# Second-direction operators and input matrices built in attention, S5 states summed before the output product, gates stored as a row

## Chip, cores and metric

One core of one Trainium2 chip runs the whole model in one launch. Times are device microseconds of that core; where runs are named, the number is the median of several executions of the same program.

## What is computed

The reference is a two-layer hybrid backbone over 1024 latent tokens and 256 context tokens of width 1024. `c` and `c_ctx` are two conditioning vectors; each layer turns both into shift, scale and gate (`ada_mod`).

```python
for layer in range(2):
    shift_x, scale_x, gate_x = ada_mod(c, ada_w[layer], ada_b[layer])        # silu(c) @ w + b, three parts
    shift_c, scale_c, gate_c = ada_mod(c_ctx, ada_w[layer], ada_b[layer])
    hx = rms_norm(x) * (1 + scale_x) + shift_x                                # hc likewise from the context
    if layer % 2 == 0:
        oc, ox = even_mixer(hc, hx, ...)   # grouped-query attention beside a bidirectional RG-LRU
    else:
        oc, ox = odd_mixer(hc, hx, ...)    # bidirectional grouped S5, then a GLU
    x = x + gate_x * ox
    if layer == 0:
        xc = xc + gate_c * oc
return rms_norm(x, final_norm_w)

def s5_direction(u, ab, bb, c, h0, reverse):          # 64 groups of 16 channels, 64 complex states each
    bu = einsum('blgj,gpj->blgp', u, bb)               # real and imaginary part
    s_re, s_im = complex_scan(ab, bu, h0, reverse)
    return einsum('blgp,gjp->blgj', s_re, c_re) - einsum('blgp,gjp->blgj', s_im, c_im)
```

`bb` (the input matrix) is the discretised `b`: `bb_re = f_re*b_re - f_im*b_im`, `bb_im = f_re*b_im + f_im*b_re`. The S5 runs forward and backward (d = 0 and 1), and the outputs are added.

## The kernel before

The projections and the output products work on float32 values that are split into a high and a low part (names ending in `h` and `l`, or `hh`, `hl`, `whi`, `wlo`), with three matmuls each. The kernel passes through these stages:

1. Norm, modulation and S5 parameters (to about 95 us).
2. Layer 0's input projections with the RG-LRU (about 95 to 405 us). TensorE's program order there is written out by hand in the string `PJ` (L857), a list of jobs with a number of steps each: `u` (RG-LRU input of a channel block), `r` (its gate matrices), `q` (queries, keys and values), `g` (gate path) and `a`, the modulation matrices of both layers (`ada`, L206). `ada` goes over eight chunks of 512 columns. A chunk is eight matmuls of 128x32 by 128x512 that fall in turn on four column groups of the array; between two of them TensorE may be given to other jobs. The result goes to SBUF as `admr`, and `part2` of the chunk before runs when two matmuls of the next are done. For a gate chunk `part2` multiplies `admr` with `selb`, which selects one condition and copies its row to 128 partitions, adds the bias on VectorE (`gt_g`) and stores 128 equal rows in `gd`; for layer 0 it does so once for each of the two conditions, out of a PSUM tag with two buffers that the chunks' sums share.
3. Attention (about 476 to 836 us): 16 units (two halves of the heads for each of eight query tiles) of ten key tiles, 160 iterations in all, every engine's program order written by hand. In an iteration TensorE transposes the exponentials (`tp`), ScalarE copies them to `pth`, VectorE makes `ptl`, TensorE multiplies with the values (`av`). `score_gen` makes the next unit's scores. Between these, steps of other generators are run: `post` (gate, output projection, residual `xr`, norm) and, from unit 2 on, two steps of `tg`, the generator `operators` on GpSimd. For each of eight channel groups f it makes the rotation tables of both directions (`tab_gen`: 8 blocks a group, each with two sums, whose halves are copied in reversed order into the same tile by GpSimd, L1238 and L1240) and the output operators `ca` of direction 0 (`op_gen`: two of 128x576 a group, three instructions each), and stores them to DRAM. The norm of a finished query tile (`norm_gen`, L1125) takes the rsqrt by Newton steps on GpSimd and multiplies `xr` by it on GpSimd (`xn`), then TensorE transposes `xn`.
4. The transition: weight splits and the input product of layer 1.
5. The S5 loop (L1880 on), f = 0 to 7, in it i = 0 to 7 for direction i // 4 and a pair of channel groups i % 4. TensorE's stream is filled with the next group's `u` and the `g` products (`fm`). `v_mm` multiplies `U` (read back from DRAM after a reordering store `usd`) with the input operator; `rot` (VectorE) turns `v` by the tables into `t1`, turns the scanned `z` of the step before back into the state `st` of two halves, and scans; `y_mm` multiplies `tm` with `U` and both halves of both directions' states with the operators `ca`. `x_gen` makes the next group's input matrix `xe`, `x2` on VectorE, `c_gen` the operators `ca` of direction 1 on VectorE, `c_sign` a sign on ScalarE; direction 0's `ca` are loaded by `c_load`.
6. GLU, output projection and final norm.

SP issues the DMAs; outside the hand-ordered blocks a scheduler orders them, and inside they stand where the code puts them. Helper `tt` (L77) records all two-tensor operations, so these are told apart by their tiles.

## Time and profile before

| | us |
|---|---|
| runs | 1480.28, 1482.72, 1492.19 (median 1482.72) |
| profiled execution | 1477.37 |
| its span, first to last instruction | 1475.6 |

The granted TensorE clock was 0.969 of full speed over the span. A row of the profile gives an engine's busy time; PE is the matmul stream of TensorE, PEld its weight loads (which overlap), DVE is VectorE, ACT ScalarE, POOL GpSimd, SP the engine that issues the DMAs. In rows of groups, `out<-in` names the tiles, then come shapes, count, busy time with the mean in nanoseconds, and the idle time of the engine just before them with what ended it.

### The profile page before, as it was taken

Reading aid. Unit: us, or ns where it says so; the run is one execution under the profiler, and the core shown is the slowest. Engines: PE = TensorE matmul, PEld = TensorE weight load, DVE = VectorE, ACT = ScalarE, POOL = GpSimd, SP = SyncE. Lnnn points to the kernel's source line nnn. Section 1 sums busy time; section 2 is a strip of 40 time slices with the busy share of each in tenths; the row PEclk is TensorE's granted clock in tenths of the full one; section 3 lists DMA queues with packets and bytes.
Section 4 is the critical chain, followed back from the end, with each engine's and each line's share of the span. In section 5 each row is a group of like instructions: output and inputs, shape, how many; then the busy total and the mean of one; then the engine's idle time right before and its main releaser. Section 6 shows DMA issues by size and latency. Waiting matters only on the chain.

```text
span 1475.6 us, 22202 instructions
## 1 busy us (share of the span) xinstructions
PE 1358.0 (92%) x7680; PEld 1117.8 (76%) x7680; DVE 1057.3 (72%) x2302; ACT 785.8 (53%) x1397; POOL 365.9 (25%) x576
## 2 busy tenths in 40 slices
PE   4699869999998999999999789999999999999996
PEld 1477648688886777887777677888888878888885
DVE  7576784878675877788887769999999983332235
ACT  4757865784656655656666445555555652222222
POOL 1030000000102488888985300000000000101153
PEclk8899979999999999999999999999999989999998
DMA  8343325444215444445432567778777873232412
GB/s 304 128 156 120 102 69 162 133 154 129 70 42 162 109 132 134 137 124 143 124 112 86 187 179 217 222 211 222 203 211 214 247 203 125 64 94 79 143 58 86
DMA packets 213153, 213.78 MB, mean 145 GB/s; under 512 B 47792, under 2 KB 170288, under 8 KB 212784
## 3 DMA queue, kind: packets, MB, share of 16 engines
q1 hardware_dynamic: 213040, 212.36, 48.3%
q8 instruction: 61, 1.00, 0.3%
q14 instruction: 52, 0.43, 0.1%
HBM read 147.89 MB, written 64.42 MB: 144 GB/s over the span
## 4 chain that ended last, share of the span: by engine, by line
PE 56%; DVE 17%; ACT 8%; issue 8%; POOL 6%; DMA 5%; SPq 0%; DVEq 0%; POOLq 0%; ACTq 0%
PE fm L1409 13%; PE fm L193 4%; PE fm L195 4%; PE fm L194 4%; PE tp L936 3%; PE v L1409 2%; PE v L1636 2%; PE op L1682 2%; PE wps L1409 2%; PE y L1682 2%; PE pS L914 2%; POOL xo L77 2%; DVE S L917 2%; PE op L1105 2%; PE op L1109 2%
## 5 line engine op out<-in xcount | busy, mean ns | idle before, releaser
L937 ACT ACTIVATE pth<-tp 128x512 fp32r<-128x512 f32 x160 | 95.4, 598 | 118.5 <-PE tp L936 114.2
L77 POOL TENSOR_TENSOR zl<-sgl,zh 128x512 fp32r<-128x512 f32 x8 | 10.4, 1296 | 477.7 <-DMA wst<-in_glu_w 377.6
L77 DVE TENSOR_TENSOR ptl<-tp,pth 128x512 fp32r<-128x512 f32 x160 | 109.5, 686 | 25.8 <-ACT pth L937 25.2
L1409 PE MATMUL fm<-hh,whi 128*128 128x512 f32 (+1 forms) x312 | 119.5, 383 | 2.7 <-ACT ut L1584 2.7
L1409 PE MATMUL fm<-hl,whi 128*128 128x512 f32 (+1 forms) x312 | 119.9, 384 | 1.0 <-POOL hl L77 1.0
L1409 PE MATMUL fm<-hh,wlo 128*128 128x512 f32 (+1 forms) x312 | 117.3, 376 | 0.0
L195 PE MATMUL fm<-hh,wlo 128*128 128x512 f32 (+1 forms) x288 | 104.1, 361 | 6.6 <-DVE wlo L77 6.6
L193 PE MATMUL fm<-hh,whi 128*128 128x512 f32 (+1 forms) x288 | 106.2, 369 | 3.2 <-DVE sg L548 1.8
L936 PE MATMUL tp<-ident,S 128*128 128x128 f32 x672 | 101.9, 274 | 5.6 <-DVE q L77 2.1
L77 DVE TENSOR_TENSOR wlo<-wst,whi 128x512 fp32r<-128x512 f32 x98 | 68.5, 721 | 52.1 <-ACT whi L1402 41.3
L194 PE MATMUL fm<-hl,whi 128*128 128x512 f32 (+1 forms) x288 | 103.8, 361 | 1.0 <-DVE hl L487 0.9
L936 PEld LDWEIGHTS tp<-ident,S 128*128 128x128 f32 x672 | 82.6, 140 | 29.2 <-ACT S L925 2.8
L925 ACT ACTIVATE S<-S,mx 128x1280 f32<-128x1280 f32 (+1 forms) x80 | 95.2, 1190 | 9.4 <-DVE S L917 9.3
L917 DVE TENSOR_SCALAR_CACHE_REDUCE S<-pS,mx 128x512 f32<-128x512 f32 (+1 forms) x128 | 78.4, 614 | 21.4 <-PE pS L915 13.7
L914 PE MATMUL pS<-k,q 128*128 128x512 f32 (+1 forms) x208 | 82.7, 402 | 11.7 <-DVE S L917 11.0
L175 POOL CAST v<-vs 128x256 fp32r<-128x256 f32 x5 | 2.1, 417 | 321.4 <-DMA gd<-gt_g 290.5
L193 PE MATMUL fm<-whi,hh 128*128 128x256 f32 x240 | 70.7, 295 | 2.5 <-ACT up L669 2.5
L915 PE MATMUL pS<-k,q 128*128 128x512 f32 (+1 forms) x208 | 71.5, 351 | 0.0
L944 PE MATMUL av<-pth,v 128*128 128x512 f32 x160 | 71.0, 444 | 0.0
L194 PE MATMUL fm<-wlo,hh 128*128 128x256 f32 x240 | 68.9, 287 | 1.4 <-DVE wlo L77 1.4
L193 PEld LDWEIGHTS fm<-hh,whi 128*128 128x128 f32 x288 | 55.7, 193 | 18.7 <-issue 4.6
L1409 PEld LDWEIGHTS fm<-hh,whi 128*128 128x128 f32 x312 | 60.0, 192 | 11.7 <-ACT ut L1584 3.0
(494 smaller groups left out, 4130.7 us busy)
## 6 DMA issues: line engine op xcount, KB each, us to landing
adw<-in_ada_w SPq DMA_DIRECT2D x48, 512.0 KB, 4.7
tab<-tabd SPq DMA_DIRECT2D x64, 320.0 KB, 5.1
tabd<-tab SPq DMA_DIRECT2D x64, 160.0 KB, 2.6
wst<-in_ev_w_in SPq DMA_DIRECT2D x36, 256.0 KB, 3.2
wst<-in_od_w_in SPq DMA_DIRECT2D x32, 256.0 KB, 4.2
tmd<-ks SPq DMA_DIRECT2D x16, 512.0 KB, 4.8
wst<-in_glu_w SPq DMA_DIRECT2D x32, 256.0 KB, 2.8
usd<-ut SPq DMA_DIRECT2D x8, 768.0 KB, 4.7
```

The costliest lines, as they stand in the source:

```text
L77: e.tensor_tensor(o, a, b, op=op)
L193: T.matmul(ps, l[0], r[0], start=first, stop=False)
L194: T.matmul(ps, l[0], r[1], start=False, stop=False)
L195: T.matmul(ps, l[1], r[0], start=False, stop=last)
L914: T.matmul(pS[:, :n], q1[:, a], k1[:, h, c0:c0 + n], start=True, stop=False)
L915: T.matmul(pS[:, :n], q2[:, a], k1[:, h, c0:c0 + n], start=False, stop=True)
L917: V.tensor_scalar(P[a][:, c0:c0 + n], pS[:, :n], -0.125, prev[a], op0=ALU.mult, op1=ALU.min, accum_out=mx[:, a, b:b + 1])
L925: S.activation(s, s, AF.Exp, bias=nb, scale=-1.0, accum_out=sm)
L936: T.transpose(ps[:, 128 * a:128 * a + 128], P[a][:, 128 * kt:128 * kt + 128], ident)
L937: S.activation(parts[0], ps, AF.Copy)
L944: T.matmul(av, v2[:, kt, h], pt[0], start=first, stop=False)
L1409: T.matmul(ps, w[k][a], r(k, b), start=k == 0 and i == 0, stop=k == 7 and i == 2)
```

## The change

- Gates as a row: one matmul with `sel` gives both conditions' rows; `gd` holds one row each, which the loads copy to 128 partitions (`gB`, `g1`). `selb` is gone. `ada` has four weight buffers in place of two and loads four ahead; `part2` of a chunk runs after all eight matmuls of the next; in `PJ` the `a` steps of a chunk stand together as `a:10`.
- Attention: GpSimd's `operators` now makes `ca` of both directions and, in a new `x_gen(f)`, the input matrices of both directions, stored in `xd`. The reversed halves of the tables are made on ScalarE by `mirror()`, at the earliest two iterations after the sum. `xn` of the norm is made by ScalarE. `t_split` takes the high part of the RG-LRU's product on ScalarE for the later units and stands two iterations behind the load. `tg` gets three steps instead of two in four of a unit's ten iterations.
- S5: `c_gen`, `c_sign` and `x_gen` are gone; `xe`, `x2` and all four `ca` are loaded. In `rot` VectorE adds the two halves of the state into `sb` and `y_mm` has one matmul in place of two for each direction.

Both halves of a state were multiplied with the same operator, so their sum can be taken before the product.

```diff
-    gd = dr.tile([3, 128, D], F32, name="gd")
+    gd = dr.tile([3, D], F32, name="gd")
...
-            for cond in range(2 - l):
-                ps = pp.tile([128, 512], F32, name="gt_p", tag=tag, bufs=pb)
-                T.matmul(ps, selb[:, cond], m, start=True, stop=True)
-                g = pq.tile([128, 512], F32, name="gt_g", tag="sg")
-                tt(V, g, ps, bb, ALU.add)
...
-                Q.dma_start(gd[2 * l + cond, :, c], g)
+            n = 2 - l
...
+            ps = pp.tile([128, 512], F32, name="gt_p", tag=tag, bufs=pb)[0:n]
+            T.matmul(ps, sel[:, 0:n], m, start=True, stop=True)
+            tt(V, g, ps, bb, ALU.add)
...
+            Q.dma_start(gd[2 * l:2 * l + n, c], g)
...
-                if prev is not None and h == 1:
+                if prev is not None and kk == 7:
                     part2(*prev)
...
-    jobs = dict(a=ada(prg, pgp, [(0, 4), (0, 5), (1, 0), (1, 4), (1, 1), (1, 2), (1, 3), (1, 5)], 2, "ad", 2, 2))
+    PJ = ("u0:26 u1:26 r0:1 q0:2 r0:2 q0:2 r0:1 q0:2 u2:16 r0:4 a:11 r0:5 u2:3 q0:8 r1:1 u2:1 q0:16 u2:5 r1:6 q0:8 r1:3 a:10 "
+          "q0:8 r1:2 u2:1 r1:1 r2:1 q0:21 r2:2 q0:14 a:10 u3:24 g0:5 r2:3 u3:2 r2:1 g0:2 r2:3 g0:5 a:10 g0:13 g1:8 r2:2 "
...
+    jobs = dict(a=ada(prg, pgp, [(0, 4), (0, 5), (1, 0), (1, 4), (1, 1), (1, 2), (1, 3), (1, 5)], 2, "ad", 4, 4))
...
-    Q.dma_start(gB, gd[0:2].rearrange("c p n -> p c n"))
+    Q.dma_start(gB, gd[0:2].unsqueeze(0).to_broadcast([128, 2, D]))
...
+    def t_split(X, e=S):
+        split(*X["mr"], X.pop("rn"), e, G)
...
-            tt(G, xn, xr, r.to_broadcast([128, D]), ALU.mult)
-            for _ in range(NW):
+            yield
+            S.activation(xn, xr, AF.Copy, scale=r)
+            for _ in range(NW - 1):
                 yield
...
             tt(G, o, o, tb, op)
-            r = tab[:, :, c, 0:80][:, :, ::-1]
-            if c:
-                G.tensor_scalar(r, o, -1.0, None, op0=ALU.mult)
-            else:
-                G.tensor_copy(r, o)
+            mirrors.append((now[0] + 2, tab, c, None if c == 0 else (d, f, q)))
...
+    def mirror():
+
+        while mirrors and mirrors[0][0] <= now[0]:
+            _, tab, c, to = mirrors.pop(0)
+            S.activation(tab[:, :, c, 0:80][:, :, ::-1], tab[:, :, c, 80:160], AF.Copy, scale=-1.0 if c else 1.0)
...
-    def op_gen(f, PP, c, h):
+    def op_gen(f, d, PP, c, h):
...
+    def x_gen(f):
...
+        for i, op in enumerate((ALU.add, ALU.subtract)):
+            tt(G, x[:, i], bc[:, i], (FR, FRs)[i], ALU.mult)
+            tt(G, t, bc[:, 1 - i], (FIs, FI)[i], ALU.mult)
+            yield
+            tt(G, x[:, i], x[:, i], t, op)
+            if i:
+                Q.dma_start(xd[f].rearrange("p a n -> p (a n)"), x.rearrange("p a d g c -> p (a d g c)"))
+            yield
...
+            for d in range(2):
...
+                for h in range(2):
+                    yield from tab_gen(f, E, M, d, h)
+                    if h == 0:
+                        G.tensor_scalar(c[:, 0], c[:, 0], sgp, -1.0, op0=ALU.mult, op1=ALU.mult)
+                    yield from op_gen(f, d, PP, c, h)
+            yield from x_gen(f)
...
-                    run(tg, 2)
+                    mirror()
+                    run(tg, 2 + (i % 3 == 0))
...
-        def x_gen(X, e):
...
-        def c_gen(X, h):
-            X["CA"][1, h] = ca = pg.tile([128, 4, 9, 16], F32, name="ca", tag="ca", bufs=6)
-            return cprod(ca, X["PP"], 1, h, slice(8, None, -1), X["c"][:, 0], X["c"][:, 1], ALU.subtract, 2)
...
-                X0["St"][p0, d0] = s = pg.tile([128, 2, 2, 128], F32, name="st", tag=f"st{d0}", bufs=3 if d0 else 4)
+                s = pg.tile([128, 2, 2, 128], F32, name="st", tag="st", bufs=2)
                 tt(V, s if d0 == 0 else s[:, :, :, ::-1], zz[:, :, :, 31:159], tab0, ALU.mult)
+                X0["St"][p0, d0] = o = pg.tile([128, 2, 128], F32, name="sb", tag=f"sb{d0}", bufs=3 if d0 else 6)
+                tt(V, o, s[:, 0], s[:, 1], ALU.add)
...
-                    for c in range(2):
-                        T.matmul(y[:, i], ca.rearrange("p t c -> p (t c)"), St[p, d][:, c, i], start=False, stop=d + c == 2)
+                    T.matmul(y[:, i], ca.rearrange("p t c -> p (t c)"), St[p, d][:, i], start=False, stop=d == 1)
...
                 if i < 2:
-                    ck = c_gen(X, i)
-                elif 2 < i < 7:
+                    c_load(X, 1, i)
+                if 2 < i < 7:
```

## Rows read from the trace of the kernel before

**Rows 1.** The page, busy time of each engine (share of span, instructions).

```profile
PE 1358.0 (92%) x7680; PEld 1117.8 (76%) x7680; DVE 1057.3 (72%) x2302; ACT 785.8 (53%) x1397; POOL 365.9 (25%) x576
```

**Rows 2.** Windows: stretch, length, busy PE, PEld, DVE, ACT, POOL, clock, DMA share, GB/s.

```profile
95.00:217.00 122.00, 99.06 (x535) 79.87 (x533) 91.94 (x156) 82.36 (x100) 0.00 (x0) 0.90 0.35 112
217.00:405.00 188.00, 181.03 (x1112) 148.07 (x1112) 134.49 (x256) 117.94 (x182) 4.52 (x8) 0.98 0.42 129
502.00:826.00 324.00, 311.41 (x1750) 253.79 (x1748) 253.14 (x633) 192.52 (x339) 254.92 (x459) 1.00 0.41 117
973.27:1014.99 41.72, 41.72 (x282) 36.52 (x281) 39.83 (x85) 23.33 (x53) 0.00 (x0) 1.00 0.76 217
```

**Rows 3.** TensorE's instructions in time near 217 us: start, us, [wait before].

```profile
217.06 2.07 PE L235 MATMUL gt_p<-admr,selb 128*128 128x512 f32 x2 [9.60 <-DVE gt_g L77]
```

**Rows 4.** TensorE's instructions in time, 255 to 290 us.

```profile
259.43 1.06 PE L255 MATMUL adps<-adw,scc 128*32 128x512 f32 x8
...
276.09 1.04 PE L255 MATMUL adps<-adw,scc 128*32 128x512 f32 x2
```

**Rows 5.** TensorE's groups by shape, 95 to 405 us.

```profile
L255 PE MATMUL adps<-adw,scc 128*32 128x512 f32 x128 | 26.4, 638 | 0.6 <-DMA adw<-in_ada_w 0.6
...
L235 PE MATMUL gt_p<-admr,selb 128*128 128x512 f32 x12 | 7.8, 737 | 11.1 <-DVE gt_g L77 11.1
```

**Rows 6.** GpSimd's groups by shape, 455 to 880 us.

```profile
L77 POOL TENSOR_TENSOR tab<-EEf,MMf 128x160 f32<-128x160 f32 x64 | 29.7, 464 | 0.0
...
L77 POOL TENSOR_TENSOR cb<-cb,ct 128x576 f32<-128x576 f32 x16 | 22.8, 1428 | 1.0
L1238 POOL TENSOR_SCALAR tab<-tab 128x160 f32<-128x160 f32 x32 | 20.0, 625 | 2.8
L77 POOL TENSOR_TENSOR cb<-PPa,bca 128x576 f32<-128x576 f32 x16 | 19.2, 1203 | 0.0
...
L77 POOL TENSOR_TENSOR xn<-xr,rs_yn 128x1024 f32<-128x1024 f32 x8 | 15.2, 1894 | 0.0
...
L1240 POOL COPY tab<-tab 128x160 f32<-128x160 f32 x32 | 10.1, 317 | 2.0
```

**Rows 7.** Waits, 476 to 836 us: total us, times, longest.

```profile
ACT pth L937 <- PE tp L936: 110.7, 91, 3.3
POOL xr L77 <- DVE o L77: 33.3, 10, 8.5
```

**Rows 8.** ScalarE's groups by shape: S5 (880 to 1200 us), then attention (476 to 836).

```profile
L1510 ACT ACTIVATE bcc<-bcc,nsg 128x128 f32<-128x128 f32 x7 | 2.9, 409 | 0.0
...
L1131 ACT ACTIVATE xn<-xr 128x1024 f32<-128x1024 f32 x9 | 9.5, 1057 | 0.2 <-POOL xr L77 0.2
```

**Rows 9.** TensorE's instructions in time, 690 to 735 us.

```profile
706.22 0.66 PE L1149 MATMUL tp<-ident,xn 128*128 128x128 f32 x4 [1.05 <-POOL xn L77]
```

**Rows 10.** Tile `at` (min/median/max ns); VectorE's groups, 476 to 836 us.

```profile
L77 DVE TENSOR_TENSOR at<-at,gat x16: 412/416/1591, 491.3 to 829.1; 128x256 f32<-128x256 f32 x16
...
L77 DVE TENSOR_TENSOR mal<-at,mah 128x256 fp32r<-128x256 f32 x16 | 10.4, 651 | 0.5 <-ACT mah L1070 0.5
```

**Rows 11.** Chain of work in order of time, 960 to 1020 us: start, us, what.

```profile
964.34 0.89 PE y L1682 x8
...
973.27 2.31 PE fm L1409 x10
...
1014.99 2.31 PE fm L1409 x10
```

**Rows 12.** VectorE's groups by shape, 973.27 to 1014.99 us.

```profile
L77 DVE TENSOR_TENSOR ca<-ca,pt 128x576 f32<-128x576 f32 x2 | 1.5, 758 | 0.1
```

**Rows 13.** SP's issue of `U`; its landing (us); TensorE's first product on it.

```profile
991.99 0.36 SPq L1593 DMA_DIRECT2D U<-usd  x1
...
U<-usd SPq DMA_DIRECT2D x7, 768.0 KB, 5.1
...
997.96 0.70 PE L1636 MATMUL v<-U,Wd 128*128 128x160 f32 x4
```

More of the change, by code (lines that the diff above doesn't have):

```diff
@@ L102, in _body @@
     Q.dma_start(scc, A["cc"])
-    selb = cst.tile([128, 2, 128], F32, name="selb")
-    G.tensor_copy(selb, sel.unsqueeze(2).to_broadcast([128, 2, 128]))
     adab = cst.tile([128, 2, 24], F32, name="adab")
@@ L1080, in t_mix @@
         t = X["t"]
-        X["mr"] = mh, ml = tuple(pb.tile([128, 4, 128], F32R, name=n, tag=n, bufs=2) for n in ("mrh", "mrl"))
+        X["mr"] = tuple(pb.tile([128, 4, 128], F32R, name=n, tag=n, bufs=2) for n in ("mrh", "mrl"))
         if t < 9:
@@ L1200, in step @@
                     t_mix(X)
+                    t_split(X, G)
                     ctx_mix(X)
@@ L1304, in _body @@
             for i in range(10):
+                now[0] += 1
                 pt = pt_T(X, h, i, tuple(pb.tile([128, 512], F32R, name=n, tag=n, bufs=3) for n in ("pth", "ptl")))
@@ L1356, in _body @@
         all_(tg)
+        now[0] += 2
+        mirror()
         while pend:
@@ L1471, in _body @@
         pg = pool("s5g", side="right", es=es_5)
-        FR, FI, FRs, FIs = (FX[:, i] for i in range(4))
         def s_load(f):
             X = dict(f=f)
-            X["b"] = pg.tile([128, 2, 2, 8, 16], F32, name="bcb", tag="bcb", bufs=1)
-            Q.dma_start(X["b"], A["s5bc"][:, f, 0:2])
+            X["xe"] = xe = pg.tile([128, 272], F32, name="xe", tag="xe", bufs=2)
+            Q.dma_start(xe[:, 0:256], xd[f, :, 0])
+            V.memset(xe[:, 256:272], 0.0)
+            x2 = pg.tile([128, 256], F32, name="x2", tag="x2", bufs=1)
+            Q.dma_start(x2, xd[f, :, 1])
+            X["x"], X["x2"] = (t.rearrange("p (d g c) -> p d g c", d=2, g=8) for t in (xe[:, 0:256], x2))
             X["PP"] = pg.tile([128, 2, 2, 8, 9], F32, name="PPf", tag="PPf", bufs=2)
@@ L1854, in _body @@
         X = s_load(0)
-        s_load2(X)
         ev = u_ev(X)
-        x_gen(X, V)
         ev(256, ua)
```

101 lines of the change are left out of this document (42 added, 59 removed), and 3 rows, old and new, of the table PJ.

## The prediction

> **What bounds the kernel now.** I read the page first, then the table of windows, then in each window the view that says what its busiest engine waits for. The page's first row says that TensorE is busy 92% of the span and VectorE 72%, GpSimd a quarter [rows 1]; such shares mix stages, so the windows come next. The reader is to see four different things there [rows 2]. From 95 to 217 us (input projections with the RG-LRU) no engine is full: 99.06 of 122 us TensorE. From 217 to 405 us TensorE is full (181.03 of 188). In attention (502 to 826 us) TensorE has 311.41 of 324 us, and GpSimd, which the page makes look idle, has 254.92. In the S5 loop one group f takes 41.72 us, TensorE has all of them and VectorE 39.83.
>
> So work taken from TensorE after 217 us, in attention or in S5 shortens the kernel, if the next engine lets it: in S5 that is VectorE, in attention GpSimd.
>
> **Part 1: gates as a row, and `PJ` regrouped.** TensorE's long wait between 95 and 405 us is L235 waiting for VectorE's `gt_g`: its matmul at 217.06 us comes after a wait of 9.6 us [rows 3], and the groups give 11.1 us of such idle time in front of L235 in all [rows 5]. The cause is in `part2`: for layer 0 the loop over `cond` takes a second PSUM buffer of two, so the second matmul must wait until VectorE has added the first, and VectorE has a whole RG-LRU chain in front of that addition. The new `part2` has one matmul for both conditions, so the wait has no cause left: 11.1 us.
>
> The ada matmuls themselves: a burst of 8 records (4 matmuls on the four column groups) takes 1.06 us and a burst of 2 records takes 1.04 [rows 4]. A burst of one matmul thus costs as much as a burst of four. Before, the 128 records come in 23 bursts, 26.4 us together [rows 5]; after, `a:10` runs a chunk's 8 matmuls in a row, two bursts of four, so 8 x 2 x 1.06 = 17 us: 9.4 us less. The gate matmuls fall from six to four: a third of 7.8 us [rows 5] is 2.6 us.
>
> Together 23 us at most, and 0 at least, since a TensorE program order with larger blocks can meet new waits for the RG-LRU chain. What falls before 217 us is worth little, because TensorE idles there anyway; the long wait ends at 217 us [rows 3], at the door of the full stretch, and most of the bursts lie behind it. I take 14 us. The loads change too: four 512 KB buffers instead of two, all of a chunk fetched while the chunk before is multiplied. It is hidden behind the blocks between two chunks (eight chunks in the 310 us from 95 to 405 us); uncovered, a chunk would wait for its four loads.
>
> The smaller `gd` (rows instead of 128 copies) saves stores that nobody waits for: 0. `selb` likewise.
>
> **Part 2: attention.** GpSimd loses the mirrored halves of the tables (20.0 + 10.1 us) and `xn` (15.2 us): 45 us [rows 6]. It gains the operators of the second direction, 16 x (2 x 1.20 + 1.43) = 61 us from the same shapes [rows 6], and `x_gen`, 48 instructions of 128x256. There is no such row; the neighbours are 0.46 us for 160 columns and 1.43 for 576 [rows 6], which bound it at 22 and 69 us; on the line between them 256 columns cost about 0.68, 33 us. (Five casts that leave and eight small scalings that come about cancel.) Net +49 us: GpSimd goes from 255 to 304 of 324 us, 94%. It was free to wait: 33.3 us of its idle time are waits for the output projection's product [rows 7], and these shrink as it comes later. The two new steps out of three extra slots (`run(tg, 2 + (i % 3 == 0))`) give 336 slots for 344 steps, so 8 steps (one operator's last part and `x_gen(7)`, about 8 us) are left for after the last unit.
>
> ScalarE gains 64 mirrors. The nearest row is 128x128 SBUF to SBUF at 0.41 us [rows 8], so 26 us, between 13 (half of it) and 52; `xn` costs 8 x 1.06 = 8.5 us by the square of the same tile [rows 8]. It has 110.7 us of waits for TensorE's transposes in this stage [rows 7] as cover. What is queued behind a waiting ScalarE instruction is `pth`, and behind `pth` VectorE's `ptl` and TensorE's next product. Two of the moved instructions can wait: a mirror for its sum on GpSimd (put two iterations later: 160 iterations in the 360 us of [rows 7], so some 4.5 us), and `xn` for GpSimd's rsqrt. Before, TensorE already waits for `xn` (the 1.05 us at 706.22 [rows 9], GpSimd having put operators in between); after, `xn` skips GpSimd's queue but the rsqrt stands later in it. I put these against each other, and charge +3 us for the stage (from -4 to +20), and +1 us for the leftover GpSimd work in front of the splits of the next stage, where TensorE waits for the last tile's norm anyway (0 to +8).
>
> One more thing can make VectorE slower here. Its 128x256 multiplication of two SBUF tiles takes 0.41 us at best, 1.59 at worst [rows 10]. It runs 16 times, as does the subtraction `mal` of the same shape, 0.65 us in the mean [rows 10]. If such a mean excess, some 0.2 us, grows with GpSimd's share (304/255), that is about 1 us in all, inside the +3. The Trainium skill ("SBUF — State Buffer", "Who interferes with whom") says that a VectorE instruction with two SBUF inputs and a GpSimd instruction that reads SBUF shut each other out for the whole instruction; the spread of this row agrees. By that rule at its strictest, each of the 32 meets a GpSimd instruction of up to 1.4 us, and the stage is some 30 us longer instead of 1: this is rival B's mechanism by another road.
>
> **Part 3: S5.** In `y_mm`, the four matmuls on the states' two halves become two per channel group: 8 records, 0.89 us in the chain, become 4 [rows 11]. Two channel groups per `y_mm`, four `y_mm` per f: 8 x 0.445 = 3.56 us per f. TensorE's period is the distance from 973.27 to 1014.99, 41.72 us, gapless [rows 2, 11]; it becomes 38.2.
>
> VectorE per f: `c_gen` goes, six instructions of 128x576, the last two 1.5 us [rows 12], 4.5 us in all; `x_gen` goes, six of 128x256 at 0.42 [rows 10], 2.5 us. The sum of two states comes eight times: 128x256, 0.42 us by the same row, plus what it loses because it follows its own input; I take 0.46, 3.7 us. So 39.8 - 7.0 + 3.7 = 36.5 us busy, and about 1 us of gaps between instructions: 37.5 of 38.2. The added sum lies between product and scan in all eight steps while `c_gen` and `x_gen` leave only i = 0 to 2, so VectorE falls behind TensorE in i = 3 to 7 and catches up in i = 0 to 2. The period is bounded by 38.2 (TensorE alone) and 41 (little of it comes through). I take 38.5: 3.25 us x 8 = 26 us, of at most 28.5.
>
> DMA: per f two more 288 KB operators and 128 KB less, 5% of what 217 GB/s move in 41.72 us [rows 2]; with the shorter period the share goes from 0.76 to about 0.87. What is late next is U: its load is issued at 991.99, takes 5.1 us, lands at 997.1, and the matmul on it starts at 997.96 [rows 13]. One `y_mm` lies in between, so that matmul would start 0.9 us earlier, just when U lands. I count this within the 38.5.
>
> **Sum.** -14 (part 1) +3 +1 (part 2) -26 (part 3) = -36 us. The profiled execution took 1477.4 us (span 1475.6 and 1.8 around it): 1441. The runs' median, 1482.7, lies 5.3 us above that execution, so 1447.
>
> **Rivals.**
> A. S5 gives its gain back. U lands later under the higher DMA share, or VectorE, with under 1 us to spare, sets the period. For it: both margins are under 1 us. Against: VectorE never waits for long in the trace and is not TensorE's releaser there. At 40 us a period the gain is 14 instead of 26 us: 1459.
> B. GpSimd becomes the bound of attention. For it: 94% in an in-order queue with waits left in it. If half of the 33.3 us of waits stay [rows 7], it needs 321 of 324 us, and 8 more at the end; its lateness then reaches ScalarE through rsqrt and mirrors: attention +15 to +20 instead of +4: 1461.
> C. Part 1 brings nothing, since the RG-LRU chain sets the pace of the shorter order: 14 us lost, 1461. Against: the stretch from 217 us on is full.
> D. It ends slower: each of the 64 mirrors stops ScalarE until GpSimd has made its sum, and `pth` behind it stops TensorE. At w us a mirror the loss is 64 w: 0.56 us eats the whole 36, and from 0.8 us on the kernel is over 1% slower; at 1 us it takes 1447 + 64 = 1511. For it: the mirror follows its sum by only two iterations while GpSimd is nearly full. Against: the 110.7 us of ScalarE's own idle time.
>
> **How the numbers follow.** About 1% (15 us) is what a measurement of this kernel can tell from no change. Forecast 0.58 (own range 1434 to 1458), A 0.14, B 0.14, C 0.07, D 0.05, and 0.02 for two of A, B, C at once. The forecast, A, C and most of B lie below 1468; so faster 0.82. Within 1%: the rest of B with two rivals at once and half of D: 0.13. Slower 0.05. The range for 8 in 10 reaches from 1430 (23 us in part 1, 28 in S5) to 1468.
>
> **What would show it.** Right: no wait of L235's gate matmul for `gt_g`; ada bursts of 8 records only; in S5 v-matmul to v-matmul over one f about 38.5 us, with 4 records where 8 were, TensorE still full and VectorE above 95%; GpSimd near 300 us in attention and ScalarE's waits there naming GpSimd a few times, not 64. Wrong: an attention stage longer by over 10 us with ScalarE waiting for `tab` or `rs_yn` (B, D); TensorE waiting for U each f (A); the full stretch after 217 us with new waits for `ri` (C).

## The result, and the profile after

The changed kernel takes 1492.44 us (median of 20 runs, 1485.52 to 1504.56) against 1480.98 before (20 runs, 1478.43 to 1492.19). The ratio is 1.0079, 95% interval 1.0061 to 1.0096: slower by 0.8%, where 1447 was forecast (1430 to 1468). The profiled execution has 1489.97 us, a span of 1488.2 and a granted clock of 0.956, against 0.969 before.

The first line of the page of the profile, to be read beside [rows 1]:

```profile
PE 1336.6 (90%) x7420; PEld 1100.7 (74%) x7420; DVE 1035.8 (70%) x2268; ACT 810.5 (54%) x1470; POOL 412.5 (28%) x602
```

TensorE is 21.4 us less busy and the span is 12.6 us longer, so its idle time grew by 34 us. The windows that answer to [rows 2] (the last one is again one period of S5):

```profile
95.00:217.00 122.00, 103.30 (x578) 88.33 (x577) 87.89 (x151) 83.81 (x101) 0.00 (x0) 0.90 0.31 104
217.00:400.00 183.00, 171.71 (x1077) 144.66 (x1075) 138.45 (x262) 120.72 (x187) 4.54 (x8) 0.95 0.40 124
502.00:826.00 324.00, 304.10 (x1696) 246.83 (x1694) 249.78 (x618) 212.13 (x404) 282.43 (x460) 0.99 0.48 143
1010.50:1050.90 40.40, 38.79 (x250) 33.16 (x249) 35.23 (x77) 22.54 (x52) 0.00 (x0) 0.99 0.82 234
```

S5 is as drawn: TensorE 38.8 us per f in place of 41.7, VectorE 35.2 in place of 39.8. But now TensorE has gaps there, in attention, and behind 217 us.

To place the time I cut each execution at five events: the first matmul of the RG-LRU's gates (`gps`), the first and the last `pth`, the first and the last `v` product of S5. The table gives the us between them in one profiled execution. The same code, in several profiles, gave 315 to 320 us for the projections, 380 to 384 for attention (in e13 and e16, which share it, 381.5 and 386.1), 62 to 65 for the transition, 313 to 322 for S5; smaller differences are not read.

| | to gps | projections | attention | transition | S5 | rest |
|---|---|---|---|---|---|---|
| before | 127.0 | 327.7 | 369.9 | 52.5 | 324.0 | 274.5 |
| changed | 129.3 | 320.0 | 380.5 | 64.0 | 317.3 | 277.1 |
| difference | +2.3 | -7.7 | +10.6 | +11.5 | -6.7 | +2.6 |

The sum is +12.6. Two stages gave back what two others gained.

**Projections.** TensorE's modulation matmuls and its longest waits, 95 to 400 us, then the same wait for `ri` before:

```profile
L253 PE MATMUL adps<-adw,scc 128*32 128x512 f32 x128 | 18.2, 694 | 0.0
```

```profile
PE gps L192 <- ACT ri L697: 17.1, 6, 4.8
PE fm L192 <- ACT qr L817: 8.5, 3, 3.2
```

```profile
PE gps L193 <- ACT ri L699: 8.7, 5, 4.4
```

The bursts cost 18.2 us in place of 26.4 [rows 5], and no wait for `gt_g` is left. But ScalarE's `ri` is waited for 8.4 us longer, and `qr` anew for 8.5.

**Attention.** ScalarE's waits for GpSimd, first to last `pth` (before, neither instruction was ScalarE's):

```profile
ACT xn L1143 <- POOL rs_yn L77: 17.8, 7, 4.0
...
ACT tab L1248 <- POOL tab L77: 3.1, 4, 1.0
```

**Transition.** The last input matrix on GpSimd, SP's queue, ScalarE's and TensorE's first instruction on the new weights; then the same load of before:

```profile
839.41 0.74 POOL L77 TENSOR_TENSOR xx<-xx,xt 128x256 f32<-128x256 f32 x1
840.18 0.33 SPq L1286 DMA_DIRECT2D xd<-xx  x1
842.55 1.68 SPq L1428 DMA_DIRECT2D wst<-in_od_w_in  x2
846.72 0.63 ACT L1439 ACTIVATE whi<-wst 128x512 fp32r<-128x512 f32 x1 [10.03 <-DMA wst<-in_od_w_in]
850.16 0.58 PE L1446 MATMUL fm<-hh,whi 128*128 128x256 f32 x1 [8.61 <-ACT hh L172]
```

```profile
826.53 0.94 SPq L1391 DMA_DIRECT2D wst<-in_od_w_in  x2
```

GpSimd works without a gap to 840.1 us, 10.4 us past the last `pth`; before, its operators ended 28.1 us ahead of it. The weights' load is issued 16 us later.

**S5.** The chain of work of one f (start, us, what), and the first product on the new `U`, to be read beside [rows 11, 13]:

```profile
1011.69 0.45 PE op L1690 x4
...
1038.72 5.27 DMA usd<-ut
1044.06 5.10 DMA U<-usd
```

```profile
1049.30 0.78 PE L1644 MATMUL v<-U,Wd 128*128 128x160 f32 x4 [1.61 <-DMA U<-usd]
```

The output product has 4 records in 0.45 us where it had 8 in 0.89. The chain now runs through the store and the load of `U`, and TensorE waits for it in six of the seven f that follow the first, 1.2 to 2.3 us each.

### The profile page after: what moved, and what is told of

It reads as the page before. It is cut to its first block, busy times and chain, and to the rows that moved or that the text cites. A ratio compares the mean times of both kernels' runs of the same rounds, so it can differ in the third digit from the quotient of the medians.

```text
span 1488.2 us, 21859 instructions
## 1 busy us (share of the span) xinstructions
PE 1336.6 (90%) x7420; PEld 1100.7 (74%) x7420; DVE 1035.8 (70%) x2268; ACT 810.5 (54%) x1470; POOL 412.5 (28%) x602
## 4 chain that ended last, share of the span: by engine, by line
PE 41%; DVE 19%; DMA 11%; ACT 10%; POOL 9%; issue 9%; SPq 1%; DVEq 0%; ACTq 0%; POOLq 0%
PE fm L1446 7%; PE fm L192 3%; PE fm L194 3%; PE fm L193 3%; PE tp L934 2%; DMA usd<-ut 2%; PE v L1446 2%; DMA U<-usd 2%; PE wps L1446 2%; POOL xo L77 2%; POOL cb L77 2%; PE adps L253 1%; PE op L1446 1%; PE pS L912 1%; PE op L1106 1%
## 5 line engine op out<-in xcount | busy, mean ns | idle before, releaser
L77 POOL TENSOR_TENSOR zl<-sgl,zh 128x512 fp32r<-128x512 f32 x8 | 10.4, 1295 | 473.5 <-DMA wst<-in_glu_w 373.3
L1446 PE MATMUL fm<-hl,whi 128*128 128x512 f32 (+1 forms) x312 | 121.6, 390 | 2.2 <-POOL hl L77 2.2
L934 PE MATMUL tp<-ident,S 128*128 128x128 f32 x672 | 102.8, 276 | 11.5 <-DVE h1s L1158 3.7
L934 PEld LDWEIGHTS tp<-ident,S 128*128 128x128 f32 x672 | 82.9, 141 | 36.5 <-issue 4.5
L193 PE MATMUL fm<-hl,whi 128*128 128x512 f32 (+1 forms) x288 | 105.1, 365 | 0.8 <-DVE hl L485 0.8
L912 PE MATMUL pS<-k,q 128*128 128x512 f32 (+1 forms) x208 | 82.8, 402 | 11.3 <-DVE S L915 10.7
L1634 ACT ACTIVATE z<-z 64x256 f32<-64x256 f32 x64 | 26.7, 417 | 106.5 <-DVE z L1676 103.7
L1446 PEld LDWEIGHTS fm<-hh,whi 128*128 128x128 f32 x312 | 61.4, 197 | 18.1 <-ACT hh L172 9.0
```

The costliest lines, as they stand in the source:

```text
L77: e.tensor_tensor(o, a, b, op=op)
L193: T.matmul(ps, l[0], r[1], start=False, stop=False)
L912: T.matmul(pS[:, :n], q1[:, a], k1[:, h, c0:c0 + n], start=True, stop=False)
L934: T.transpose(ps[:, 128 * a:128 * a + 128], P[a][:, 128 * kt:128 * kt + 128], ident)
L1446: T.matmul(ps, w[k][a], r(k, b), start=k == 0 and i == 0, stop=k == 7 and i == 2)
```

## The experiments

The times are medians of several executions. The ratio is to the kernel before on the same chip, with its 95% interval. The lengths of the stages come from one profiled execution of each run.

| run | us | ratio | projections | attention | transition | S5 |
|---|---|---|---|---|---|---|
| e1 late stores | 1483.95 | 1.0027 (1.0010 to 1.0045) | 315.7 | 383.3 | 62.4 | 318.5 |
| e2 norm on VectorE | 1499.56 | 1.0140 (1.0104 to 1.0176) | 319.6 | 396.2 | 63.0 | 312.7 |
| e3 u in halves | 1494.18 | 1.0091 (1.0062 to 1.0120) | 315.5 | 380.6 | 63.6 | 323.8 |
| e4 old order, gate row | 1490.69 | 1.0064 (1.0042 to 1.0086) | 319.8 | 380.3 | 64.2 | 322.4 |
| e5 rsqrt first | 1493.80 | 1.0109 (1.0071 to 1.0146) | 315.7 | 389.7 | 62.7 | 318.4 |
| e6 x on VectorE | 1469.02 | 0.9925 (0.9900 to 0.9949) | 319.8 | 376.9 | 53.6 | 316.1 |
| e7 early u | 1480.96 | 0.9998 (0.9984 to 1.0012) | 315.1 | 381.5 | 65.1 | 309.0 |
| e8 part 1 alone | 1475.17 | 0.9963 (0.9943 to 0.9983) | 320.0 | 372.3 | 52.2 | 323.8 |
| e9 light GpSimd | 1513.88 | 1.0242 (1.0216 to 1.0267) | 315.2 | 384.8 | 52.7 | 354.5 |
| e10 S5 ca on GpSimd | 1499.12 | 1.0132 (1.0107 to 1.0158) | 319.7 | 372.0 | 52.2 | 353.5 |
| e11 S5 ca and x on GpSimd | 1500.07 | 1.0132 (1.0108 to 1.0157) | 319.6 | 370.7 | 51.4 | 352.0 |
| e12 = e6 + e7 | 1467.67 | 0.9921 (0.9895 to 0.9948) | 315.2 | 376.4 | 53.9 | 314.4 |
| e13 = e12, xn on GpSimd | 1474.19 | 0.9971 (0.9951 to 0.9992) | 320.0 | 381.5 | 54.7 | 311.6 |
| e14 = e12, mirrors on GpSimd | 1489.85 | 1.0064 (1.0042 to 1.0086) | 316.9 | 396.3 | 54.1 | 313.6 |
| e15 = e12, both on GpSimd | 1497.13 | 1.0115 (1.0085 to 1.0145) | 320.4 | 402.5 | 54.2 | 313.6 |
| e16 = e13, early ca | 1477.16 | 0.9980 (0.9963 to 0.9997) | 317.1 | 386.1 | 54.1 | 316.4 |
| e17 sum alone | 1492.04 | 1.0077 (1.0047 to 1.0107) | 319.7 | 370.3 | 51.4 | 345.5 |
| e18 no sum | 1495.32 | 1.0102 (1.0085 to 1.0119) | 319.8 | 382.9 | 64.7 | 320.5 |

### The transition: e1 and e6

```diff
+                (G if f == 7 else Q).dma_start(xd[f].rearrange("p a n -> p (a n)"), ...)   # e1; the last cad and tabd stores likewise
```

> The changed kernel, but the stores of the last operators, of the last input matrix and of the last mirrored tables are issued by GpSimd instead of SP. Measured in the changed kernel: from the last pth (829.8 us) to the first v product of S5 (893.8) 64.0 us, against 52.5 before; the first whi of the transition waits 10.0 us for its load, whose issue stands on SP at 842.6 behind those stores. Theory (SP is held in order by stores that wait for GpSimd): the load is issued before 835 us, the stretch falls to 53 to 55 us, the kernel to about 1482. Rival (GpSimd's leftover work to 840 us itself is late, for the splits that follow on it): the stretch stays at 60 to 64 us and the kernel within 3 us of 1492.

In e1 the weights' load is issued early, but the next one is not. SP's queue, GpSimd's last stores, and ScalarE's wait:

```profile
827.95 1.07 SPq L1428 DMA_DIRECT2D wst<-in_od_w_in  x2
...
839.68 1.26 POOL L1252 DMA_DIRECT2D tabd<-tab  x2
841.61 0.80 SPq L1416 DMA_DIRECT2D h<-h1d  x2
846.37 2.22 ACT L172 ACTIVATE hh<-h 128x1024 fp32r<-128x1024 f32 x2 [10.34 <-DMA h<-h1d]
```

The stretch stays at 62.4 us: SP's order alone is not the cause, and the theory as I put it fell. SP's longest wait in that stretch says what its load of `h` (L1416) stood behind:

```profile
SPq L1416 <- DMA xd<-xx: 11.4, 1, 11.4
```

That is the store of GpSimd's last input matrix. `h` does not read `xd`, so the likely reason is that its tile takes over SBUF of attention, which has to be free first; this was not tried by itself. The kernel as a whole was 8 us faster than the changed one, and this stretch explains 1.6 of it; the rest is not explained.

```diff
-            yield from x_gen(f)          # in operators()
+                    if i == 2:
+                        x_gen(N, V)      # in the S5 loop, as before
```

> The changed kernel, but the input matrices are made by VectorE in S5 again: GpSimd loses x_gen (32.9 us of its work in attention), S5 two loads of 128 KB each f, VectorE gains 2.5 us each f. Measured so far: first to last pth 380.5 us, from there to S5's first v 64.0 (62.4 to 64.2 in four profiles), S5 first to last v 317.3 (312.7 to 322.4). Theory (GpSimd's load is the cause in both stages: its operators end at 840 us, and the transition's loads and splits cannot start before): operators end before the last pth, the transition falls to 53 to 56 us, attention to 370 to 376. S5: VectorE has 37.7 of some 40 us a period, no slower than 40.7. Kernel about 1476. Rival (something else in the transition, such as the order of SP's loads): it stays at 60 us or more.

GpSimd's last operator and SP's load of the weights in e6:

```profile
801.93 1.44 POOL L77 TENSOR_TENSOR cb<-cb,ct 128x576 f32<-128x576 f32 x1
...
827.68 0.94 SPq L1427 DMA_DIRECT2D wst<-in_od_w_in  x2
```

The operators end 22 us ahead of the last `pth`, and the transition is 53.6 us: 10.4 of the 11.5 us are back (attention, at 376.9 us, came out just above its 370 to 376). So GpSimd's late end, by whichever road, is shown to be the cause. Attention lost 3.6 us less, S5 did not slow, and the kernel is 23 us faster than the changed one and 0.75% faster than before.

### Attention: e2, e5, e9 and e13 to e15

```diff
-                        post.e = V if u == 14 else G
+                        post.e = V                       # e2
```

> The changed kernel, but the whole norm of a query tile (rsqrt and the product xn) runs on VectorE for every tile, as it does for the last but one already. Measured in the changed kernel: first to last pth 380.5 us against 369.9 before; ScalarE waits 17.8 us in 7 waits for GpSimd's rsqrt before xn, and 4.4 us for sums to mirror. Theory (the rsqrt stands late in GpSimd's full queue and stops ScalarE, and with it pth): these waits go, first to last pth falls to 368 to 372 us, the kernel to about 1482. Rival (VectorE has no room for 8 more norms of about 2 us, or it is GpSimd's access to SBUF that slows VectorE): the stage stays at 377 us or more.

The waits for rsqrt are gone, and attention is 15.7 us longer than in the changed kernel. The rival held in its first half: the norms now stand in VectorE's order beside `S` and `ptl`, and TensorE's waits for `S` rise from 9.3 to 19.6 us.

```diff
-                    mirror()                             # e5: these two lines
-                    run(tg, 2 + (i % 3 == 0))            #     moved behind post.step(...)
```

> The changed kernel, but in each attention iteration the steps of the output projection and norm stand ahead of the iteration's operator steps and mirrors, so that GpSimd takes rsqrt and the residual sums before the two or three operator steps of the same iteration. First to last pth: 380.5 us in the changed kernel (380.3 to 383.3 in the three profiles so far with the same attention code), 369.9 before. Theory (rsqrt stands behind operator steps in GpSimd's full queue): ScalarE's 17.8 us of waits for rs_yn fall below 8, first to last pth to 370 to 376 us. Rival (GpSimd is simply full, so that whatever it does first, something else is late): the waits move to mirrors or to the residual, the stage stays within 3 us of 380.

The waits for `rs_yn` stay at 16.7 us, those for `tab` rise from 3.1 to 8.5, the stage to 389.7. The theory fell: this order does not bring the rsqrt earlier. The waits move to the mirrors, as the rival said, but the stage is 9 us longer and not within 3.

```diff
+                    if d:
+                        continue                         # e9: no op_gen for direction 1
-            yield from x_gen(f)
```

> The changed kernel, but in attention GpSimd makes only the tables and direction 0's operators, as before (direction 1's operators are made in the S5 loop by GpSimd, which is idle there, the input matrices by VectorE there, and u is put forward as in the run with the early u). Mirrors, xn and the late high parts stay on ScalarE. So GpSimd has some 100 us less to do in attention than in the changed kernel and 55 less than before. First to last pth: 369.9 us before, 372.3 with part 1 alone, 380.5 in the changed kernel, 376.9 without x_gen. Theory (GpSimd's load, through rsqrt and sums that come late, is the whole loss): 368 to 372 us, no wait of ScalarE for rs_yn over 1 us. Rival (ScalarE's 30 us more of mirrors and xn stand in front of pth): 374 us or more with GpSimd at 70%.

The theory fell: the stage has 384.8 us although GpSimd is busy 226 us only. But the rival's reason is not the one either: ScalarE waits 18.9 us for rsqrt. GpSimd's waits say why, in e9 and then in the changed kernel:

```profile
POOL tab L77 <- DMA tabd<-tab: 32.1, 12, 6.6
```

```profile
POOL tab L77 <- DMA tabd<-tab: 3.4, 1, 3.4
```

With fewer operators in between, the tables come round faster than the mirrors, two iterations late, and their stores free a table's buffer. GpSimd stands 32.1 us in front of such buffers, and rsqrt behind it. So this run does not tell load from order; the next three do better. (Its S5 of 354.5 us is the case of e10 below.)

```diff
-            S.activation(xn, xr, AF.Copy, scale=r)       # e13, e15
+            tt(G, xn, xr, r.to_broadcast([128, D]), ALU.mult)
-            mirrors.append((now[0] + 2, tab, c, ...))    # e14, e15
+            G.tensor_scalar(r, o, -1.0, None, op0=ALU.mult)   # or G.tensor_copy(r, o)
```

> The changed kernel with input matrices on VectorE and early u (1467.7 us; first to last pth 376.4 there), and with the norm's xn back on GpSimd as before. Then no ScalarE instruction waits for rsqrt; GpSimd gains 15 us. Theory (ScalarE, in order, stands before xn until GpSimd has made the rsqrt, 9 to 19 us in the profiles, and pth stands behind it): first to last pth falls to 370 to 373 us, the kernel to 1462 to 1464. Rival (the loss comes from ScalarE's 64 mirrors, or from GpSimd's load): the stage stays at 375 us or more.

> The same base (input matrices on VectorE, early u), xn on ScalarE, but the mirrored halves made by GpSimd as before: ScalarE loses 64 instructions of 0.33 us and some 3 us of waits for sums, GpSimd gains 30 us (to some 320 of 377). Theory (the waits for rsqrt are the loss, and a fuller GpSimd makes them longer): first to last pth 376 to 385 us. Rival (ScalarE's mirrors are the loss): 370 to 373.

> The same base with both xn and mirrors on GpSimd, so that attention differs from before by direction 1's operators on GpSimd alone (some 335 of 375 us). Theory (waits of ScalarE for GpSimd are the loss): 369 to 373 us for first to last pth although GpSimd is at 90%; operators end near the last pth. Rival (GpSimd's load is the loss): 376 or more, and a longer transition.

GpSimd's busy time from first to last `pth` and the length of the stage, in the order of the first:

| | GpSimd busy | attention | ScalarE waits for rsqrt, mirrors' sums |
|---|---|---|---|
| before | 273.9 | 369.9 | 0, 0 |
| e8 | 274.0 | 372.3 | 0, 0 |
| e12 | 289.6 | 376.4 | 10.5, 2.9 |
| e13 | 304.1 | 381.5 | 0, 5.9 |
| changed | 311.0 | 380.5 | 17.8, 3.1 |
| e14 | 318.0 | 396.3 | 29.6, 0 |
| e15 | 333.5 | 402.5 | 0, 0 |

Where ScalarE no longer waits, TensorE does. Its first wait in e15, 448 to 852 us (before, 3.0 us in four waits):

```profile
PE tp L1150 <- POOL xn L77: 27.3, 8, 5.0
```

So neither of ScalarE's new tasks is the loss by itself; taking either of them back makes the stage longer. The loss comes with GpSimd's load, and most of it through the norm, whichever engine stands behind the norm's rsqrt. From before and e8 to e15 GpSimd has 59.6 us more work and attention is about 31 us longer. `x_gen` alone, which is all that the changed kernel has over e12 in this stage, is 21.4 and 4.1 us.

The price of a us is not constant, and load is not all of it. e13 and e16 (304 us of GpSimd) take as long as the changed kernel (311) or longer, while e14, with 14 us more than e13, takes 14.8 us more. e15 differs from before by more than direction 1's operators: `t_split` and the third steps of `tg` are those of the changed kernel. Which of GpSimd's instructions costs most stays open.

My theory for e13 fell, and the rival that names GpSimd's load held there. In e14 the waits for rsqrt grew as its theory said, but the stage is 11 us above its range. In e15 the rival held for attention; the transition did not grow, since the operators end 21 us ahead of the last `pth`.

The prediction had another road: GpSimd's reads could hold up VectorE. VectorE's busy time from first to last `pth` is 290.0 us before, 293.4 in the changed kernel and 290.6 in e15, so that was at most 3.4 us. The product that grew, to be read beside [rows 10]:

```profile
L77 DVE TENSOR_TENSOR at<-at,gat x16: 416/731/1544, 485.1 to 834.7; 128x256 f32<-128x256 f32 x16
```

### S5: e3, e7, e16, e17, e18

```diff
-            for c0, n in ((256, 512), (768, 512), (0, 256)):     # e3, in u_gen
+            for c0, n in ((0, 256), (256, 512), (768, 512)):
+                        Q.dma_start(usd[f]...[:, j:j + 4], ut[:, j:j + 4])   # each half when it is there
```

> The changed kernel, but the context columns of u are made first and ut is stored in two halves, each as soon as it is there, so that the last store before the load of U has half the bytes. Measured in the changed kernel: from v(0) of one f to that of the next 40.7 us in the mean (first to last v of S5 317.3 us), TensorE waits 1.2 to 2.3 us for U in each f, and a store of ut lands 6.0 us after its issue. Theory (the round trip of U through DRAM has become the bound): the waits for U go, the period falls to 38.5 to 39.2 us, first to last v to 302 to 308, the kernel to about 1480. Rival (the DMA engines' share, 0.82, or VectorE sets the period): the wait moves to another load or to VectorE, the period stays above 40.2.

After the first f TensorE still waits 5.7 us for `U`, and now 7.7 us for `ut`, whose copies hold the PSUM buffers. The period, from one issue of the load of `U` to the next, is 41.6 us. Nothing was gained; on the theory it is inconclusive.

```diff
-                step(6, ug, gg)                # then 5 and 5; u ends in i = 4
+                step(n1, ug, gg)               # 7, 6, 5 for i < 4, then 4, 4, 4; u ends in i = 3
```

> The changed kernel, but in the S5 loop the next group's u product is put further forward (18 matmuls in each of i = 0 to 3 in place of 16 in i = 0 to 4), so that it ends half a step, some 2.4 us, earlier, and the gate product follows with 12 a step. Measured so far: TensorE waits 1.2 to 2.3 us for U in each f, mean period 40.7 us; storing ut in two halves did not shorten it (its waits moved to ut). Theory (U's store and load take 11 to 12 us and the stretch that covers them became 0.9 us shorter): the waits for U go, the period falls to 38.6 to 39.3, first to last v to 303 to 310 us. Rival (the DMA share of 0.83, or VectorE's rot behind i = 4 to 7): the period stays above 40.2 with other waits.

TensorE's waits for `U` in S5 in e7, and in the changed kernel (the wait of the first f, which before has too, is 3.9 and 3.2 us of them):

```profile
PE v L1644 <- DMA U<-usd: 7.4, 4, 3.9
```

```profile
PE v L1644 <- DMA U<-usd: 13.9, 7, 3.2
```

From one issue of the load of `U` to the next (mean of six) there are 39.05 us, against 40.71 in the changed kernel and 41.58 before; S5 is 309.0 us and the kernel 11.5 us faster than the changed one. The waits after the first f fall from 10.7 to 3.5 us. The round trip was the bound, and most of its waits can be covered.

```diff
-                        T.matmul(y[:, i], ca..., St[p, d][:, i], start=False, stop=d == 1)       # e18; e17 the reverse, on e8
+                    for c in range(2):
+                        T.matmul(y[:, i], ca..., St[p, d][:, c, i], start=False, stop=d + c == 2)
```

> The kernel before with part 1 and, in S5, the state sum with one matmul per direction; direction 1's operators and the input matrices stay on VectorE in S5, so attention is that of before. Part 1 alone gave 1475.2 us with 323.8 us from first to last v. Theory (VectorE, 40 us busy in a period of 41.7, takes over as the bound as soon as 3.4 us of sums are added): the period rises to 43 to 44.5 us, S5 to 335 to 345, the kernel to 1488 to 1497: the S5 part pays only with the operators taken off VectorE. Rival (the matmuls saved count more): S5 at 320 or less.

> The changed kernel without the state sum: two matmuls for each direction in y_mm as before; operators and input matrices still come from attention by loads. VectorE then has about 33 us per f, TensorE 41.7. Theory (TensorE's matmuls set the period once the sum is gone, and the longer cover hides U): no waits for U, the period 41.5 to 42, S5 at 322 to 328 us, 5 to 10 more than in the changed kernel. Rival (loads set the period, whatever TensorE does): S5 stays at 313 to 320 us.

The windows of e17 and of e18, five periods of S5 each (columns as in [rows 2]):

```profile
935.00:1155.00 220.00, 197.19 (x1217) 168.10 (x1214) 215.27 (x455) 114.66 (x265) 0.00 (x0) 0.97 0.71 204
```

```profile
935.00:1155.00 220.00, 219.16 (x1471) 191.94 (x1470) 175.19 (x370) 119.88 (x271) 0.00 (x0) 1.00 0.82 230
```

Alone, the sum makes VectorE the bound (215.3 of 220 us, period 44.24); without it, TensorE is (219.2 of 220, period 41.73). Both theories held by the periods (S5 of e17 is 0.5 us above its range, that of e18 1.5 us below). Neither half of part 3 shortens the period of 41.58 us without the other, and together they meet `U` at 40.7.

```diff
+                    c_load(N, 1, i - 6)                  # e16, with bufs=8
```

> As the run with xn on GpSimd, and direction 1's operators ca are loaded two steps before the loop of their f, into eight buffers in place of six. In the runs so far TensorE waits 6 to 7 us in the last f for a ca whose load SP issued late. Theory: this wait goes, S5 first to last v falls by 4 to 6 us against that run. Rival (the load only takes the DMA engines from U and the tables at the end of each f): U's waits grow and S5 stays.

TensorE's waits for `ca` in the last f of the changed kernel, then what is left in e16:

```profile
1189.26 1.10 PE L1560 MATMUL kp<-ca,xe 128*32 128x128 f32 x14 [6.82 <-DMA ca<-cad]
1202.96 1.10 PE L1560 MATMUL kp<-ca,xe 128*32 128x128 f32 x16 [4.89 <-issue]
```

```profile
1193.31 1.11 PE L1575 MATMUL kp<-ca,xe 128*32 128x128 f32 x16 [4.82 <-issue]
```

The wait for the load went (it is 4.75 us in e13, on which e16 is built), and S5 did not get shorter. Other waits of that f took its place; those for `U` did not grow (9.2 us against 11.8), so the rival's reason does not hold either.

### S5 with GpSimd: e10 and e11

```diff
-            return cprod(ca, ..., ALU.subtract, 2)
+            return cprod(ca, ..., ALU.subtract, 2, G)    # c_gen, on the kernel before with part 1, sum and early u
```

> The kernel before with part 1, the state sum and one matmul per direction in S5, direction 1's operators made by GpSimd inside the S5 loop (7.6 us of its work per f by the rates in attention), the input matrices by VectorE there, and the early u. Attention is that of before. Theory (S5's gain is real when neither U's round trip nor VectorE nor attention pays for it): S5 first to last v 302 to 310 us, attention 370 to 373, transition 52 to 53, the kernel 1452 to 1460. Rival (GpSimd beside VectorE slows VectorE's instructions with two SBUF inputs, as at was slowed in attention): VectorE's products and sums of 128x256 and 128x512 in S5 take clearly longer than 0.42 and 0.69 us and the period stays above 40 us, S5 at 318 or more.

> As the run with direction 1's operators on GpSimd inside S5, but the input matrices are made by GpSimd there too: 11.5 us of GpSimd per f by the rates in attention, VectorE 2.5 us less. Theory (VectorE then has 35 of some 39 us, and GpSimd's time is hidden): no slower than that run, S5 300 to 308 us. Rival (GpSimd's accesses cost VectorE more than the 2.5 us): S5 slower than in that run by 1 us per f, 8 us, or more.

VectorE's groups by shape over 200 us of S5 in e10, then in the changed kernel:

```profile
L77 DVE TENSOR_TENSOR st<-z,tab 128x512 f32<-128x512 f32 x34 | 29.1, 856 | 0.0
L77 DVE TENSOR_TENSOR wlo<-wst,whi 128x512 fp32r<-128x512 f32 x18 | 20.5, 1180 | 0.0
L77 DVE TENSOR_TENSOR t<-v,tab 128x320 f32<-128x320 f32 x35 | 16.8, 481 | 0.1
```

```profile
L77 DVE TENSOR_TENSOR st<-z,tab 128x512 f32<-128x512 f32 x39 | 26.7, 685 | 0.0
L77 DVE TENSOR_TENSOR t<-v,tab 128x320 f32<-128x320 f32 x40 | 19.4, 484 | 12.4 <-ACT vs L1635 6.7 <-DMA tab<-tabd 4.0 <-PE op L1690 1.6
...
L77 DVE TENSOR_TENSOR wlo<-wst,whi 128x512 fp32r<-128x512 f32 x18 | 11.6, 686 | 0.4
```

With GpSimd busy 41 of 200 us (0 in the changed kernel), `wlo` takes 1.18 us in place of 0.69 and `st` 0.86 in place of 0.69; `t` of `v`, which reads one of its inputs from PSUM, stays at 0.48. VectorE is busy 196.4 of 200 us, and S5 takes 353.5 us, 8 more than in e17, where VectorE makes these operators itself. The rival held. This agrees with the rule of the Trainium skill that I weighed in the prediction ("SBUF — State Buffer", "Who interferes with whom"): VectorE's instructions with two SBUF inputs are held off by GpSimd's reads, those with at most one (outside its two-port modes) are not. e11 is no slower, as its theory said, but its S5 of 352.0 us is far from 300 to 308, though `x_gen` too has left VectorE.

### The projections: e4 and e8

```diff
-    jobs = dict(a=ada(..., "ad", 4, 4))     # e4: old PJ, two buffers, part2 at its old place
+    jobs = dict(a=ada(..., "ad", 2, 2))
```

> The changed kernel, but with TensorE's program order of the projections, the chunks of the modulation, their two buffers and the place of part2 as before; the gates stay one row. Measured: first pth at 449.3 us in the changed kernel, at 454.7 before; the changed one lost the 11.1 us of waits for gt_g and 8.2 us of modulation matmuls, but TensorE waits 8.4 us more for ri and 8.5 us for qr. Theory (the new order met the waits that it saved; the gate's single matmul does the good): first pth at 444 to 449 us, no wait for gt_g, waits for qr gone, kernel 1487 to 1492. Rival (the order with whole chunks is what gained the 5.4 us): first pth at 452 us or later.

> The kernel before with the first part of the change alone: gates as a row, whole chunks of the modulation, the new order of TensorE in the projections. From the first matmul of the RG-LRU's gates to the first pth: 327.7 us before, 315.5 to 320.0 in the four profiles with this code. Theory (this part saves what the profiles say, and nothing later takes it back): 8 to 12 us less than before in that stretch and in the whole: about 1470. Rival (the lower clock of the changed kernel, 0.953 against 0.968, comes from this stage and eats it): about 1480.

TensorE's waits in e4 for `ri` and `qr`, to be read beside 17.1 and 8.5 us of the changed kernel:

```profile
PE gps L192 <- ACT ri L697: 10.8, 5, 4.6
PE fm L192 <- ACT qr L817: 3.2, 1, 3.2
```

With the old order and the gate row the projections take 319.8 us, as with the new order (315 to 320), so the single gate matmul does the good and whole chunks add nothing that can be told from noise. Against e4 the whole chunks save 10.6 us of bursts (28.8 us there). TensorE waits 11.6 us longer for these two, 5.5 us less elsewhere, and its clock is lower. The first `pth` is at 446.9 us, inside the theory's range; one wait for `qr` is left.

Part 1 alone gives 1475.17 us, 4.8 less than before, halfway between theory and rival. The rival has something to it: from 217 to 400 us the granted clock is 0.95 to 0.96 in the profile of the changed kernel and of all the seventeen runs with whole chunks, e8 among them, against 0.98 before and 0.99 in e4.

e12 holds the two mends that helped:

> The changed kernel with the two edits that helped: input matrices made by VectorE in S5, and the early u. Alone they gave 1469.0 and 1481.0 us, against 1492.4. Theory (they mend two different stages, transition and S5): both gains add, S5 first to last v 306 to 312 us, the kernel 1457 to 1462. Rival (with x_gen VectorE sets the period of S5): S5 stays at 315 us, the kernel at 1467 to 1470.

They don't add: 1467.67 us, S5 314.4, VectorE busy 195 of 200 us there, as the rival said. It is the fastest of all, level with e6.

## Why the prediction was wrong

The forecast was -36 us; the stages give +12.6. Of the 48.6 us between them S5 has 19.3, the transition 10.5, attention 7.6 and the projections 6.3; 4.9 lie in the first and the last stretch, where nothing was forecast and little differs.

**Part 1, -14 forecast, -7.7 in its stage, -4.8 alone.** The sizes of the terms held: the bursts gave 8.2 us of 9.4, the gate wait its 11.1, the gate matmuls 3.8 of 2.6. The step that failed is how 23 became 14: what was taken off stands for work before 217 us, while "new waits for the RG-LRU chain", named for the lower bound, were charged nothing. Those for `ri` and `qr` grew by 17 us. By e4 they and the lower clock left nothing of the bursts' gain.

(Ahead of the prediction stands that `part2` ran behind two matmuls of the next chunk, and that the tables are eight blocks a group. It is four matmuls, since a buffer holds two of the eight, and four blocks, which gives the 64 mirrors. No term hung on either.)

**Part 2, +3 forecast, +10.6.** GpSimd's added work was sized well: 412.5 against 365.9 us in the pages is +46.6, forecast +49, and `x_gen` took 0.64 to 0.75 us an instruction, forecast 0.68. (In the window of [rows 2] it is 282 us and not 304, since the operators began before 502 and ran on to 840.) The failed step is "I put these against each other": `xn` skipping the queue was to cancel the rsqrt standing later in it, so 49 us in a nearly full queue were charged almost nothing. The rsqrt comes after a dozen small GpSimd steps in a row, and ScalarE waited 17.8 us for it, where TensorE had waited 3.0 for `xn`; with `xn` back on GpSimd (e13) the stage was no shorter. This is rival B by its signs, at 10.6 us where B had 15 to 20. VectorE's part, forecast at 1 us, was at most 3.4; the 30 us of the strictest reading did not come.

**Leftover GpSimd work, +1 forecast (0 to +8), +11.5.** I counted the eight steps, found them 8 us long (they ended 10.4 us after the last `pth`), and asked only who needs GpSimd next (the splits). Who needs SP's queue behind their stores was left out, and so was what stands behind the stores themselves: 11.4 us of SP's wait in e1. D's worry was the wrong one: the 64 mirrors cost 3.1 us of waits.

**Part 3, -26 forecast, -6.7.** This is the largest miss. TensorE and VectorE came out at 38.8 and 35.2 us per f, forecast 38.2 and 36.5. The failed step is one sentence: that the matmul would start "just when U lands", counted as nothing. I moved the matmul 0.9 us up and left the landing where it was. With the DMA share at 0.82 the store took a median of 6.0 us in place of 4.7, and TensorE waited 1.2 to 2.3 us in six of seven f. Rival A named it at 40 us a period; 40.7 came. e7 shows that 39.05 was to be had. The sum had no term either for a wait on the loads of `ca` that replace `c_gen`: in the last f TensorE waits 6.8 us for one.

**What no term held.** The removed matmuls are 28.5 + 8.2 + 3.8 = 40.5 us of TensorE, but its busy time fell by 21.4. The granted clock was 0.956 in place of 0.969, which by an estimate from the two figures is 1.3% of 1358 us, 18 us. The clock was taken as given. It differs most where TensorE stood longer, as at 850 to 900 us, before and after:

```profile
850.00:900.00 50.00, 43.60 (x249) 37.15 (x250) 37.48 (x75) 21.03 (x44) 3.00 (x1) 0.94 0.62 175
```

```profile
850.00:900.00 50.00, 38.77 (x198) 34.13 (x199) 32.42 (x52) 20.37 (x35) 14.96 (x6) 0.85 0.66 203
```

TensorE's clock has two levels, 1.2 and 2.4 GHz, so the lower share means a longer time at 1.2 GHz. That the stalls are the cause was not tried by itself.

**The chances.** A and B came and C about half, and I gave 0.02 to two of them at once. Put on top of the forecast, their three prices make 1487 us, near what was measured: the mechanisms were there as rivals, and the sum left each of them out. They were not independent: each says that a margin of a few us, in a queue that is nearly full, does not hold. The outcome lies in the class "within 1%", which had 0.13. The classes do not follow from the parts, either: the forecast, A, C and more than half of B make at least 0.86 for "faster", not 0.82.

## What to carry to other kernels

Work moved to an idle-looking engine is priced in the stage where it lands, by what stands behind it in that engine's order: here 47 us of GpSimd cost 22 us in two stages. When a bound falls, the next one is a chain with a latency, and its cover shrinks with the gain: subtract before calling it hidden. Two halves of an edit may each bring nothing alone (e17, e18), so price the pair and say which half moves what.

## What the hardware showed

With GpSimd busy a fifth of the time (41 of 200 us), VectorE's subtraction `wlo` of two SBUF tiles took 1.7 times as long (0.69 to 1.18 us), and others up to 1.25 times. In attention, where most of VectorE's instructions read an input from PSUM, 37 us more of GpSimd's work went with at most 3.4 us more of VectorE's time.

The start of the program, to the first `gps` matmul, hardly differs between these kernels. It took 127 to 131 us in all profiles but one, and 138.5 in e2. There the granted clock was 0.74 and 0.78 in the first two stretches of 50 us, with TensorE busy 26.8 and 36.6 us in them; before it was 0.83 and 0.93, with 25.3 and 41.6 us. Why is not known.
